# Recurrent features: the bonus issued last, the key products on VectorE, the inverse's turning held behind the turned keys' product

## The chip, the cores and the metric

The kernel runs on one core of a Trainium2 chip. The metric is the time of the whole program on the device in microseconds, the median of several runs. One core has a matrix engine (TensorE, in the traces PE, with its weight loads as PEld), VectorE (DVE), ScalarE (ACT), GpSimd (POOL) and SyncE (SP), which here only issues transfers. Each engine works through a queue of its own in order.

## The reference

The program is two residual blocks over a sequence of 512 positions and 1024 channels. The change lies in the second block's recurrent mixer (RWKV7), 1024 channels wide in 16 heads of 64:

```python
k_mod = k * (1.0 + (a - 1.0) * k_a)          # a = sigmoid(a0 + a_low @ a2)
kk = heads(k * k_k)
kk = kk / maximum(sqrt(sum(kk * kk)), 1e-12)

def step(state, inp):
    r_t, w_t, k_t, v_t, aa_t, bb_t = inp      # aa = -kk, bb = kk * a
    sa = einsum('bhvk,bhk->bhv', state, aa_t)
    state = state * w_t + sa * bb_t + v_t * k_t
    return state, einsum('bhvk,bhk->bhv', state, r_t)
_, y = lax.scan(step, state0, ...)
y = normalize(y) * lnx_w + lnx_b
bonus = sum(r_h * k_h * r_k, axis=-1, keepdims=True) * v_h
return (y + bonus) * g
```

Everything is float32.

## The kernel before

**GEMMs.** Both blocks are mostly GEMMs over 512 positions, kept at float32 accuracy by splitting operands into a high and a low part. One step is three matmuls of 128x512 (`mm3`, L193 to L195): high weights by high and by low activations, low weights by high activations. A weight chunk is transferred to `wraw` (L161, SP's queue), ScalarE makes its high part `whi` (L173) and VectorE the low part `wlo` (L174). `K.split` (L187, L188) makes such a pair of an activation, here `rkh` and `rkl` of `rk`.

**The recurrent mixer** (function `rwkv`) has eight tiles of 128 channels, two heads each. They are worked in four blocks of two: `features` for each of the two, then `inverse` and `chain` for the pair, then the outputs. The scan over 512 positions is done in chunks of 64: within a chunk the products of keys, reading vectors and decays form small matrices ("grams"), one triangular matrix is inverted, and `chain` carries the state from chunk to chunk.

`features(i)` loads k, r and v from scratch memory, makes the decays `pd` and their inverses `ip`, `tha` (a tanh from which a follows), `kk` and the norms `dd` (eight small matmuls L975, then L977). Then come, in this order of the code: `kw` (ScalarE, L980) and the modified key `km` = kw * k (GpSimd, L982); the bonus: `rk` (VectorE, L985), its split, two matmuls with a matrix of ones per head (L988), `bv` (L990, L991) and its transfer to scratch (L992), which the outputs read much later; `kka` = (0.5 tha + 0.5) * kk (ScalarE L994, GpSimd L995); the operands `ar` (L1005 to L1011) and `bk` (L1019, L1020) in two halves; the grams (PE L1030, masked into `g` by VectorE L1033); the turned keys: `bp` = bk times the chunk's decay (VectorE L1042), four transposes on PE (L1046), `bkt` (ScalarE L1048); the transposes of v (L1052) and `sv`.

`inverse` collects the diagonal 32x32 pieces of the grams of both features in `nst` by 32 copies on GpSimd (L1074), turns them on VectorE into `nn` (L1076), scales them by the norms (L1080), and does 31 pairs of small steps (L1088, L1090), all on VectorE; then `xsc` (L1092), `xn` (L1094) and `x0` (L1096). PE's L1117 needs `xn`.

**What sets the order.** A scheduler puts the instructions of the code in order for each engine, so that GEMMs of the mixer's inputs and of attention fill PE between the small recurrent matmuls. `K.behind(a, b)` makes a follow b in that order without a semaphore between them. The tiles of `features` are `bpage` tiles, 28 slots shared in turn. PSUM banks named `sc` (two) take the recurrent products.

Of the kernel before, what the change touches and what calls it, by code (L numbers as in the profile page):

```python
# [5 lines left out]
F32 = mybir.dt.float32  # L6
# [3 lines left out]
AF = mybir.ActivationFunctionType  # L10
ALU = mybir.AluOpType
AX = mybir.AxisListType
PSUM = bass.MemoryType.PSUM
P = 128
# [839 lines left out]
def rwkv(K, hs, filler=lambda: None):  # L854
    nc = K.nc
    c = K.const
# [7 lines left out]
    nc.vector.tensor_scalar(hw0, K.v("w0", 0, 8), 0.5, None, ALU.mult)  # L864
    omh = c.tile([P, 8], F32, name="omh")
    nc.vector.tensor_scalar(omh, hka, -1.0, 1.0, ALU.mult, ALU.add)
    half = c.tile([P, 1], F32, name="half")
    nc.vector.memset(half, 0.5)
    gneps = c.tile([P, 1], F32, name="gneps")
    nc.vector.memset(gneps, 64e-5)  # L870

# [46 lines left out]
    scr = K.dram.tile([DT, 2, P, S], F32, name="rw_scr")  # L918
    for i in range(2):
# [5 lines left out]
        for u in range(4):  # L925
            ps = K.mm()
# [3 lines left out]
            t = K.page(name="gt")  # L930
# [3 lines left out]
    def v3(ap, a, b):  # L934
        return ap.rearrange("p (a b) -> p a b", a=a)

    def features(i, dd, svs):
        o = Ctx()
        k = K.bpage(name="k")
        nc.sync.dma_start(k, zscr[i])  # L940
        r = K.bpage(name="r")
        nc.sync.dma_start(r, zscr[8 + i])
        v = K.bpage(name="v")
        nc.sync.dma_start(v, zscr[16 + i])

        ww = K.wload("w_w2", i, 2 * P, "l3", K.invp, los=((slice(0, 64), slice(P, 2 * P)),))
        ps = K.bank("sc")
        nc.tensor.matmul(ps, ww[:, :P], lwp, start=True, stop=False)
        nc.tensor.matmul(ps, ww[:, P:], lwp, start=False, stop=True)
        sg = K.bpage(name="sg")  # L950
        nc.scalar.activation(sg, ps, AF.Tanh, scale=0.5, bias=hw0[:, i:i + 1])
        nc.vector.tensor_scalar(sg, sg, 1.0, None, ALU.add)
        cs = K.bpage(name="cs")
        nc.vector.tensor_tensor_scan(cs, K.keep, sg, 0.0, ALU.mult, ALU.add)
        pd = K.bpage(name="pd")
        nc.scalar.activation(pd, cs, AF.Exp, scale=-0.5 * C05)
        ip = K.bpage(name="ip")
        nc.scalar.activation(ip, cs, AF.Exp, scale=0.5 * C05)
        wh, wl = K.wload("w_a2", i, P, "l2", K.invp)
        ps = K.bank("sc")  # L960
        nc.tensor.matmul(ps, wh, al, start=True, stop=False)
        nc.tensor.matmul(ps, wl, al, start=False, stop=True)
        tha = K.bpage(name="tha")
        nc.scalar.activation(tha, ps, AF.Tanh, scale=0.5, bias=ha0[:, i:i + 1])
        o.pl = K.sm.tile([P, 8], F32, name="pl", tag="pl")
        nc.vector.tensor_copy(o.pl, v3(pd, 8, 64)[:, :, 63])

        kk = K.bpage(name="kk")
        nc.scalar.activation(kk, k, AF.Copy, scale=K.v("k_k", i))
        sq = K.bpage(name="sq")  # L970
        nc.scalar.activation(sq, k, AF.Square, scale=K.v("k_k", i))
        ps = K.bank("sc")
        for j in range(8):
            bs = slice(64, 128) if j % 2 == 0 else slice(0, 64)
            nc.tensor.matmul(ps[bs, j // 2:j // 2 + 5:4], sq[:, j * 64:j * 64 + 64], K.hcol, start=True, stop=True)  # L975
        p8 = (i % 2) * 8
        nc.vector.tensor_scalar(dd[:, p8:p8 + 8], ps[:, 0:8], 1e-24, None, ALU.max)  # L977

        w = K.bpage(name="kw")
        nc.scalar.activation(w, tha, AF.Identity, scale=hka[:, i:i + 1], bias=omh[:, i:i + 1])  # L980
        km = K.bpage(name="km")
        nc.gpsimd.tensor_tensor(km, w, k, ALU.mult)  # L982

        rk = K.bpage(name="rk")
        nc.vector.scalar_tensor_tensor(rk, r, K.v("r_k", i), km, ALU.mult, ALU.mult)  # L985
        ps = K.bank("sc")
        for j, z in enumerate(K.split(rk, "rk", K.bpage)):
            nc.tensor.matmul(ps, K.bonr, z, start=(j == 0), stop=(j == 1))  # L988
        bv = K.bpage(name="bv")
        nc.vector.tensor_tensor(bv, ps, v, ALU.mult)  # L990
        nc.scalar.activation(bv, bv, AF.Identity, bias=K.v("lnx_b", i))  # L991
        nc.sync.dma_start(scr[i, 1], bv)  # L992
        kka = K.bpage(name="kka")
        nc.scalar.activation(kka, tha, AF.Identity, scale=0.5, bias=half)  # L994
        nc.gpsimd.tensor_tensor(kka, kka, kk, ALU.mult)  # L995

        o.ar, bk = [], []
        for hf in range(2):
            ts = slice(hf * 256, hf * 256 + 256)
            ar = K.bpage(name="ar")  # L1000
            a5 = ar.rearrange("p (j c x t) -> p j c x t", j=2, c=2, x=2)
            kk4, pd4, r4 = [z[:, ts].rearrange("p (j c t) -> p j c t", j=2, c=2) for z in (kk, pd, r)]
            for e in range(2):

                nc.vector.scalar_tensor_tensor(a5[:, :, e, 1 - e, 1:], kk4[:, :, e, 1:], -1.0, pd4[:, :, e, :63],  # L1005
                                               ALU.mult, ALU.mult)
                nc.vector.tensor_tensor(a5[:, :, e, e, :], r4[:, :, e], pd4[:, :, e], ALU.mult)
            ks_ = kk[:, ts].rearrange("p (j t) -> p j t", j=4)[:, :, 0:1]
            a4 = ar.rearrange("p (j t) -> p j t", j=4)
            nc.vector.tensor_scalar(a4[:, 0:4:2, 64:65], ks_[:, 0:4:2], -1.0, None, ALU.mult)  # L1010
            nc.vector.tensor_scalar(a4[:, 1:4:2, 0:1], ks_[:, 1:4:2], -1.0, None, ALU.mult)  # L1011
            o.ar.append(ar)
            b = K.bpage(name="bk")
            b5 = b.rearrange("p (j c x t) -> p j c x t", j=2, c=2, x=2)
            kka4 = kka[:, ts].rearrange("p (j c t) -> p j c t", j=2, c=2)
            km4 = km[:, ts].rearrange("p (j c t) -> p j c t", j=2, c=2)
            ip4 = ip[:, ts].rearrange("p (j c t) -> p j c t", j=2, c=2)
            for e in range(2):
                nc.vector.tensor_tensor(b5[:, :, e, 1 - e, :], kka4[:, :, e], ip4[:, :, e], ALU.mult)  # L1019
                nc.vector.tensor_tensor(b5[:, :, e, e, :], km4[:, :, e], ip4[:, :, e], ALU.mult)  # L1020
            bk.append(b)

        o.g = [[], []]
        for hf in range(2):
            pss = [K.bank("sc") for e in range(2)]
            for j in range(4):
                cl = slice(j * P, j * P + P)
                for e in range(2):
                    rows = slice(e * 64, e * 64 + 64)
                    nc.tensor.matmul(pss[e][:, cl], bk[hf][rows, cl], o.ar[hf][rows, cl], start=True, stop=True)  # L1030
            for e in range(2):
                g = K.bpage(name="g")
                nc.vector.tensor_tensor(v3(g, 2, 256), v3(pss[e], 2, 256),  # L1033
                                        K.gmask.rearrange("p (o t) -> p o t", o=1).broadcast_to([P, 2, 256]), ALU.mult)
                o.g[e].append(g)

        o.bkt = []
        for hf in range(2):
            tp = K.bank("sc")

            bp = K.bpage(name="bp")
            nc.vector.tensor_tensor(v3(bp, 4, P), v3(bk[hf], 4, P),  # L1042
                                    o.pl[:, hf * 4:hf * 4 + 4].rearrange("p (a o) -> p a o", o=1).broadcast_to([P, 4, P]),
                                    ALU.mult)
            for j in range(4):
                nc.tensor.transpose(tp[:, j * P:(j + 1) * P], bp[:, j * P:(j + 1) * P], K.idt)  # L1046
            t = K.bpage(name="bkt")
            nc.scalar.activation(t, tp, AF.Copy)  # L1048
            o.bkt.append(t)
        tp = K.bank("sc")  # L1050
        for m in range(4):
            nc.tensor.transpose(tp[:, m * P:(m + 1) * P], v[:, m * P:(m + 1) * P], K.idt)  # L1052
        for hf in range(2):

            t5 = svs[hf].rearrange("p (j c x n) -> p j c x n", j=2, c=2, x=2)[:, :, :, i % 2]
            src = v3(tp[:, hf * 256:hf * 256 + 256], 2, P)
            nc.scalar.activation(t5[0:64, :, 0, :], src[0:64], AF.Copy)
            nc.scalar.activation(t5[64:128, :, 1, :], src[64:128], AF.Copy)
        return o

    def inverse(os_, dd):

        ip_ = K.invp
        nst = ip_.tile([P, 32, 32], F32, name="nst", tag="nst")
# [8 lines left out]
                        cl = (q % 2) * 32  # L1073
                        nc.gpsimd.tensor_copy(nst[rows, u0:u0 + 2, :], g4[rows, :, 1 - q // 2, q // 2, cl:cl + 32])  # L1074
        nn = ip_.tile([P, 32, 32], F32, name="nn", tag="nn")
        nc.vector.transpose(nn, nst.rearrange("p u t -> p t u"))  # L1076
        rd = K.sm.tile([P, 32], F32, name="rd", tag="rd", bufs=2)
        nc.vector.transpose(rd, dd)
        nc.vector.reciprocal(rd, rd)
# [5 lines left out]
        for t in range(31):  # L1085
            n, w = 31 - t, t + 1
# [20 lines left out]
        for p_, o in enumerate(os_):  # L1107
            ps = K.bank("sc")
            t2 = K.bpage(name="t2")
            for ul in range(8):  # L1110
                e, jp = ul // 4, ul % 4
# [783 lines left out]
```

## Time and profile before

| what | value |
|---|---|
| median of 3 runs | 1985.5 us (1985.28 to 1989.89) |
| the profiled execution | 1986.21 us |
| its span, first to last instruction | 1984.4 us |
| TensorE busy | 1913.7 us (96%) |
| VectorE busy | 1270.7 us (64%) |
| ScalarE busy | 888.7 us (45%) |
| GpSimd busy | 92.5 us (5%) |
| mean granted TensorE clock | 0.993 of full |

The span leaves 1.8 us of the profiled execution outside. The recurrent stage lies between about 790 and 1420 us. In it PE is busy for 597.26 of 630.00 us; what ends its idle time there is named instruction by instruction in the list of waits.

### The profile page before, as it was taken

The page shows a single profiled execution, that of the slowest core. Times are in us where ns is not written, and L with a number is a line of the kernel's source. Part 1 is how long each engine was busy: PE and PEld are TensorE (multiplying, and loading weights), DVE is VectorE, ACT ScalarE, POOL GpSimd, SP SyncE. Part 2 cuts the span into 40 slices and gives each one's busy share as a digit, 9 for nine tenths or more (in the row PEclk, how much of TensorE's full clock was granted, in tenths as well). Part 3 has the DMA queues.
Part 4 walks back from the last instruction along what each step waited for, and adds up shares of the span by engine and source line. Part 5 has one row for each costly group of instructions (what it writes and reads, how often), then busy time and mean ns, then how long its engine had stood idle before and what let it go on. Part 6 is the DMA issues. An engine that isn't in the chain of part 4 may idle for free. (4 is left out here: it accounts for less than half of the span.)

```text
span 1984.4 us, 28608 instructions
## 1 busy us (share of the span) xinstructions
PE 1913.7 (96%) x10895; PEld 1558.5 (79%) x10907; DVE 1270.7 (64%) x2307; ACT 888.7 (45%) x1607; POOL 92.5 (5%) x207
## 2 busy tenths in 40 slices
PE   9999999999999999999999999989999899999998
PEld 7888887787888888777776777767767798888886
DVE  6746776868866668685575575575466566535654
ACT  5322233326655555534445555555642344423432
POOL 0000000000000000110020020020000000000002
PEclk9999999999999999999999999999999999999999
DMA  5332365675322223643542433433554603233222
GB/s 173 97 96 96 96 204 188 209 230 182 123 85 75 83 93 125 205 117 97 166 140 102 168 110 107 155 107 117 179 173 156 196 22 98 88 101 106 96 84 87
DMA packets 98377, 254.57 MB, mean 128 GB/s; under 512 B 11200, under 2 KB 15808, under 8 KB 98240
## 3 DMA queue, kind: packets, MB, share of 16 engines
q1 hardware_dynamic: 96640, 250.46, 39.3%
q8 instruction: 86, 1.41, 0.3%
q10 hardware_dynamic: 1376, 1.50, 0.2%
q0 software_dynamic: 224, 0.79, 0.1%
q14 instruction: 51, 0.42, 0.1%
HBM read 212.59 MB, written 37.75 MB: 126 GB/s over the span
## 5 line engine op out<-in xcount | busy, mean ns | idle before, releaser
L173 ACT ACTIVATE whi<-wraw 128x1024 fp32r<-128x1024 f32 (+4 forms) x293 | 289.7, 989 | 568.0 <-PE mm L194 351.9
L174 DVE TENSOR_TENSOR wlo<-wraw,whi 128x1024 fp32r<-128x1024 f32 (+4 forms) x293 | 332.0, 1134 | 198.3 <-ACT whi L173 194.2
L193 PE MATMUL mm<-hh,whi 128*128 128x512 f32 x936 | 373.1, 399 | 3.3 <-DVE cv L1554 2.4
L194 PE MATMUL mm<-hl,whi 128*128 128x512 f32 x936 | 375.6, 401 | 0.0
L195 PE MATMUL mm<-hh,wlo 128*128 128x512 f32 x936 | 372.2, 398 | 0.0
L193 PEld LDWEIGHTS mm<-hh,whi 128*128 128x128 f32 x936 | 176.8, 189 | 41.6 <-issue 4.4
L194 PEld LDWEIGHTS mm<-hl,whi 128*128 128x128 f32 x936 | 177.0, 189 | 37.8 <-issue 1.5
L195 PEld LDWEIGHTS mm<-hh,wlo 128*128 128x128 f32 x936 | 176.9, 189 | 36.0 <-issue 2.2
L194 PE MATMUL mm<-xgl,whi 128*128 128x512 f32 x416 | 163.5, 393 | 0.3 <-DVE xgl L386 0.3
L195 PE MATMUL mm<-xgh,wlo 128*128 128x512 f32 x416 | 162.1, 390 | 0.0
L193 PE MATMUL mm<-xgh,whi 128*128 128x512 f32 x416 | 161.8, 390 | 0.2 <-ACT xgh L385 0.2
L194 PE MATMUL mm<-yl,whi 128*128 128x512 f32 (+1 forms) x256 | 98.3, 384 | 0.0
L193 PE MATMUL mm<-yh,whi 128*128 128x512 f32 (+1 forms) x256 | 98.2, 383 | 0.0
L195 PE MATMUL mm<-yh,wlo 128*128 128x512 f32 (+1 forms) x256 | 98.1, 383 | 0.0
L194 PEld LDWEIGHTS mm<-xgl,whi 128*128 128x128 f32 x416 | 78.1, 188 | 17.3 <-issue 0.7
L195 PEld LDWEIGHTS mm<-xgh,wlo 128*128 128x128 f32 x416 | 78.1, 188 | 17.1 <-issue 0.7
L193 PEld LDWEIGHTS mm<-xgh,whi 128*128 128x128 f32 x416 | 78.1, 188 | 16.7 <-ACT xgh L385 0.6
L783 DVE SCALAR_TENSOR_TENSOR adaw<-adaw,cb 128x1024 f32<-128x1024 f32 x48 | 58.6, 1221 | 34.5 <-DMA adaw<-in_w_ada 33.0
L194 PE MATMUL mm<-fal,whi 128*128 128x512 f32 (+1 forms) x176 | 67.4, 383 | 0.0
L195 PE MATMUL mm<-fah,wlo 128*128 128x512 f32 (+1 forms) x176 | 67.3, 382 | 0.0
L193 PE MATMUL mm<-fah,whi 128*128 128x512 f32 (+1 forms) x176 | 67.3, 382 | 0.0
L720 ACT ACTIVATE p<-sc,nm 128x128 f32<-128x128 f32 (+1 forms) x64 | 33.7, 527 | 55.4 <-DVE nm L717 44.6
(450 smaller groups left out, 3690.5 us busy)
## 6 DMA issues: line engine op xcount, KB each, us to landing
adaw<-in_w_ada SPq DMA_DIRECT2D x48, 512.0 KB, 3.8
wraw<-in_w_up SPq DMA_DIRECT2D x41, 512.0 KB, 3.5
wraw<-in_w_at SPq DMA_DIRECT2D x36, 512.0 KB, 3.6
wraw<-in_w_pin SPq DMA_DIRECT2D x30, 512.0 KB, 3.6
wraw<-in_w_rw SPq DMA_DIRECT2D x27, 512.0 KB, 4.1
wraw<-in_w_min SPq DMA_DIRECT2D x22, 512.0 KB, 4.0
a_scr<-aqkv SPq DMA_DIRECT2D x36, 256.0 KB, 2.1
aq<-a_scr SPq DMA_DIRECT2D x36, 256.0 KB, 3.8
```

The lines of the kernel that those rows point to most:

```text
L173: a = nc.scalar.activation(hi, raw, AF.Copy)
L174: b = eng.tensor_tensor(lo, raw, f(hi), ALU.subtract)
L193: nc.tensor.matmul(out, wh, ah, start=first, stop=False)
L194: nc.tensor.matmul(out, wh, al, start=False, stop=False)
L195: nc.tensor.matmul(out, wl, ah, start=False, stop=last)
L720: nc.scalar.activation(p[:, :nk], sc[:, :nk], AF.Exp, bias=nm, scale=scale, accum_out=sm)
L783: nc.vector.scalar_tensor_tensor(w, w, 1.0, K.cb, ALU.mult, ALU.mult, accum_out=K.ada[:, i:i + 1])
```

## The change

Four edits, all in `rwkv`. The bonus (rk, its split, the two matmuls, bv and its transfer) is moved from the middle of `features` to its end. `km` is computed on VectorE and not on GpSimd. `kka` is one VectorE instruction, (tha + 1) * kk, in the place of one on ScalarE and one on GpSimd; its missing factor 0.5 moves into the product `bk`, which becomes a scalar_tensor_tensor, and the constant `half` goes. The turning `nn` in `inverse` is ordered behind the last `bp` of each of its two features (`o.turned`).

```diff
@@ features
         km = K.bpage(name="km")
-        nc.gpsimd.tensor_tensor(km, w, k, ALU.mult)
-
-        rk = K.bpage(name="rk")
-        nc.vector.scalar_tensor_tensor(rk, r, K.v("r_k", i), km, ALU.mult, ALU.mult)
-        ps = K.bank("sc")
-        for j, z in enumerate(K.split(rk, "rk", K.bpage)):
-            nc.tensor.matmul(ps, K.bonr, z, start=(j == 0), stop=(j == 1))
-        bv = K.bpage(name="bv")
-        nc.vector.tensor_tensor(bv, ps, v, ALU.mult)
-        nc.scalar.activation(bv, bv, AF.Identity, bias=K.v("lnx_b", i))
-        nc.sync.dma_start(scr[i, 1], bv)
+        nc.vector.tensor_tensor(km, w, k, ALU.mult)
+
         kka = K.bpage(name="kka")
-        nc.scalar.activation(kka, tha, AF.Identity, scale=0.5, bias=half)
-        nc.gpsimd.tensor_tensor(kka, kka, kk, ALU.mult)
+        nc.vector.scalar_tensor_tensor(kka, tha, 1.0, kk, ALU.add, ALU.mult)
...
-                nc.vector.tensor_tensor(b5[:, :, e, 1 - e, :], kka4[:, :, e], ip4[:, :, e], ALU.mult)
+                nc.vector.scalar_tensor_tensor(b5[:, :, e, 1 - e, :], kka4[:, :, e], 0.5, ip4[:, :, e], ALU.mult, ALU.mult)
...
-            nc.vector.tensor_tensor(v3(bp, 4, P), v3(bk[hf], 4, P),
+            o.turned = nc.vector.tensor_tensor(v3(bp, 4, P), v3(bk[hf], 4, P),
...
+        rk = K.bpage(name="rk")
+        nc.vector.scalar_tensor_tensor(rk, r, K.v("r_k", i), km, ALU.mult, ALU.mult)
+        ps = K.bank("sc")
+        for j, z in enumerate(K.split(rk, "rk", K.bpage)):
+            nc.tensor.matmul(ps, K.bonr, z, start=(j == 0), stop=(j == 1))
+        bv = K.bpage(name="bv")
+        nc.vector.tensor_tensor(bv, ps, v, ALU.mult)
+        nc.scalar.activation(bv, bv, AF.Identity, bias=K.v("lnx_b", i))
+        nc.sync.dma_start(scr[i, 1], bv)
         return o
@@ inverse
-        nc.vector.transpose(nn, nst.rearrange("p u t -> p t u"))
+        ins = nc.vector.transpose(nn, nst.rearrange("p u t -> p t u"))
+        for o in os_:
+            K.behind(ins, o.turned)
```

How the instructions stand on the engines follows from the scheduler. Three places, all in the second feature of block 2; rows show line, operation, output and inputs with buffer numbers.

VectorE around `nn`, before (the two `bp` are the two halves of the feature):

```order
L1033 TENSOR_TENSOR g_8929<-sc_8918,gmask_7324 128x512
L1042 TENSOR_TENSOR bp_8932<-bk_8886,pl_8843 128x512
L1076 STREAM_TRANSPOSE nn_8992<-nst_8958 128x1024
L1042 TENSOR_TENSOR bp_8941<-bk_8898,pl_8843 128x512
L1080 TENSOR_TENSOR nn_8992<-nn_8992,rd_8994 128x1024
L1088 TENSOR_TENSOR xtmp_9001<-nn_8992,xinv_8998 128x31
L1090 TENSOR_TENSOR xinv_8998<-xinv_8998,xtmp_9001 128x31
```

The same place now (lines are those of the changed kernel: L1030 is bp, L1074 nn, L1049 rk, L1054 bv):

```order
L1021 TENSOR_TENSOR g_8910<-sc_8899,gmask_7324 128x512
L1030 TENSOR_TENSOR bp_8913<-bk_8867,pl_8838 128x512
L174 TENSOR_TENSOR wlo_11603<-wraw_11600,whi_11602 128x1024
L1030 TENSOR_TENSOR bp_8922<-bk_8879,pl_8838 128x512
L1074 STREAM_TRANSPOSE nn_8986<-nst_8952 128x1024
L1049 SCALAR_TENSOR_TENSOR rk_8939<-r_8806,vec_72,km_8856 128x512
L1080 TENSOR_TENSOR nn_8986<-nn_8986,rd_8988 128x1024
L188 TENSOR_TENSOR rkl_8943<-rk_8939,rkh_8942 128x512
L1088 TENSOR_TENSOR xtmp_8995<-nn_8986,xinv_8992 128x31
L1171 COPY rh0_7607<-ch_9152 64x256
L1090 TENSOR_TENSOR xinv_8992<-xinv_8992,xtmp_8995 128x31
L1054 TENSOR_TENSOR bv_8948<-sc_8941,v_8808 128x512
```

The second bp stands ahead of nn with a weight split between the two, and rk, rkl and bv stand behind nn among the inverse's steps. In block 3 the two bp stood ahead of nn before too; there a wlo between them is gone. In block 1 a wlo and a `zm` (L882, a GEMM's output) now stand between the two bp, in block 4 a wlo.

PE from the second L1046 on, before (v's transposes are L1052, `ch` is the chain's first product):

```order
L1046 MATMUL sc_8940<-cst_84,bp_8941 128x128 x4
L1052 MATMUL sc_8949<-cst_84,v_8813 128x128 x4
L194 MATMUL mm_11575<-hl_7034,whi_11578 128x512
L195 MATMUL mm_11575<-hh_7033,wlo_11579 128x512
L193 MATMUL mm_11575<-hh_7035,whi_11578 128x512
L1157 MATMUL ch_9158<-sv_8654,g_8913 64x64
L1157 MATMUL ch_9158<-sv_8654,g_8915 64x64
L194 MATMUL mm_11575<-hl_7036,whi_11578 128x512
L195 MATMUL mm_11575<-hh_7035,wlo_11579 128x512
```

And now, from the transposes of v (here L1040) to the bonus's first matmul (here L1052):

```order
L1040 MATMUL sc_8930<-cst_84,v_8808 128x128 x4
L195 MATMUL mm_11565<-hh_7029,wlo_11569 128x512
L193 MATMUL mm_11565<-hh_7031,whi_11568 128x512
L194 MATMUL mm_11565<-hl_7032,whi_11568 128x512
L1157 MATMUL ch_9152<-sv_8650,g_8894 64x64
L1157 MATMUL ch_9152<-sv_8650,g_8896 64x64
L195 MATMUL mm_11565<-hh_7031,wlo_11569 128x512
L193 MATMUL mm_11565<-hh_7033,whi_11568 128x512
L194 MATMUL mm_11565<-hl_7034,whi_11568 128x512
L195 MATMUL mm_11565<-hh_7033,wlo_11569 128x512
L193 MATMUL mm_11565<-hh_7035,whi_11568 128x512
L1052 MATMUL sc_8941<-rkh_8942,bonr_7329 128x512
```

The bonus's matmuls come five GEMM matmuls behind L1157; before, they stood ahead of the grams. From the first L1046 to the first L1117 PE's order now holds 19, 11, 11 and 17 more GEMM matmuls in blocks 1 to 4.

VectorE from the norms to the operands of the grams, before:

```order
L977 TENSOR_SCALAR dd_8652<-sc_8849 128x8
L1078 STREAM_TRANSPOSE rd_8994<-dd_8652 128x32
L1079 RECIPROCAL rd_8994<-rd_8994 128x32
L985 SCALAR_TENSOR_TENSOR rk_8863<-r_8811,vec_72,km_8861 128x512
L174 TENSOR_TENSOR wlo_11579<-wraw_11576,whi_11578 128x1024
L188 TENSOR_TENSOR rkl_8867<-rk_8863,rkh_8866 128x512
L990 TENSOR_TENSOR bv_8872<-sc_8865,v_8813 128x512
L1005 SCALAR_TENSOR_TENSOR ar_8879<-kk_8845,pd_8828 128x2x63
```

And now (L980 is km, L983 kka, L993 the first ar):

```order
L975 TENSOR_SCALAR dd_8648<-sc_8844 128x8
L1078 STREAM_TRANSPOSE rd_8988<-dd_8648 128x32
L1079 RECIPROCAL rd_8988<-rd_8988 128x32
L980 TENSOR_TENSOR km_8856<-kw_8854,k_8804 128x512
L983 SCALAR_TENSOR_TENSOR kka_8858<-tha_8836,kk_8840 128x512
L174 TENSOR_TENSOR wlo_11569<-wraw_11566,whi_11568 128x1024
L993 SCALAR_TENSOR_TENSOR ar_8860<-kk_8840,pd_8823 128x2x63
```

km and kka stand where rk, rkl and bv stood.

## Rows read from the trace of the kernel before

**Rows 1.** Page, part 1: span, then busy time of each engine.

```profile
span 1984.4 us, 28608 instructions
...
PE 1913.7 (96%) x10895; PEld 1558.5 (79%) x10907; DVE 1270.7 (64%) x2307; ACT 888.7 (45%) x1607; POOL 92.5 (5%) x207
```

**Rows 2.** What PE waited for, 790 to 1420 us: total us, times, longest.

```profile
PE sc L1046 <- DVE bp L1042: 6.7, 3, 2.8
PE sc L1117 <- DVE xn L1094: 4.6, 4, 1.7
PE sc L1030 <- DVE bk L1020: 3.6, 5, 1.3
...
PE sc L988 <- ACT rkh L187: 2.4, 4, 0.9
...
PE sc L988 <- DVE rkl L188: 0.6, 1, 0.6
```

**Rows 3.** Timeline, block 2, second feature: start us, duration us, engine, line, [idle before].

```profile
1021.79 0.68 DVE L1042 TENSOR_TENSOR bp<-bk,pl 128x512 f32<-128x512 f32 x1
...
1023.98 0.39 PE L195 MATMUL mm<-hh,wlo 128*128 128x512 f32 x1
...
1024.20 0.40 PE L193 MATMUL mm<-hh,whi 128*128 128x512 f32 x1
1024.81 1.91 DVE L1076 STREAM_TRANSPOSE nn<-nst 128x1024 f32<-128x1024 f32 x1 [2.34 <-POOL nst L1074]
1026.63 0.66 DVE L1042 TENSOR_TENSOR bp<-bk,pl 128x512 f32<-128x512 f32 x1
...
1027.43 0.63 PE L1046 MATMUL sc<-cst,bp 128*128 128x128 f32 x4 [2.83 <-DVE bp L1042]
...
1029.51 0.50 PE L194 MATMUL mm<-hl,whi 128*128 128x512 f32 x1
```

**Rows 4.** Timelines of blocks 1 and 4, second features: PE, then VectorE.

```profile
867.00 0.63 PE L1046 MATMUL sc<-cst,bp 128*128 128x128 f32 x4 [2.06 <-DVE bp L1042]
...
1325.65 0.63 PE L1046 MATMUL sc<-cst,bp 128*128 128x128 f32 x4 [1.85 <-DVE bp L1042]
...
1320.79 0.67 DVE L1042 TENSOR_TENSOR bp<-bk,pl 128x512 f32<-128x512 f32 x1
1322.97 1.95 DVE L1076 STREAM_TRANSPOSE nn<-nst 128x1024 f32<-128x1024 f32 x1 [1.50 <-POOL nst L1074]
```

**Rows 5.** Copies into nst: beside bp, beside wlo; then all (lines view).

```profile
1021.91 0.66 POOL L1074 COPY nst<-g 32x64 f32<-32x64 f32 x1
...
1172.38 1.20 POOL L1074 COPY nst<-g 32x64 f32<-32x64 f32 x1
...
L1074 POOL COPY nst<-g 32x64 f32<-32x64 f32 x128 | 39.8, 311 | 45.3 <-DVE g L1033 40.4
```

**Rows 6.** Timelines of PE at the first L1117 of each block.

```profile
907.10 0.69 PE L1117 MATMUL sc<-xn,g 32*32 32x32 f32 x32 [1.69 <-DVE xn L1094]
...
1061.63 0.69 PE L1117 MATMUL sc<-xn,g 32*32 32x32 f32 x32 [0.92 <-DVE xn L1094]
...
1212.81 0.69 PE L1117 MATMUL sc<-xn,g 32*32 32x32 f32 x32 [0.98 <-DVE xn L1094]
...
1358.74 0.69 PE L1117 MATMUL sc<-xn,g 32*32 32x32 f32 x32 [1.03 <-DVE xn L1094]
```

**Rows 7.** Lines view, 790 to 1420 us: busy us, mean ns | idle before.

```profile
L982 POOL TENSOR_TENSOR km<-kw,k 128x512 f32<-128x512 f32 x8 | 11.0, 1374 | 137.4 <-ACT kw L980 93.6 <-DMA aq<-a_scr 24.5 <-DVE rd L1079 9.7
...
L1020 DVE TENSOR_TENSOR bk<-km,ip 128x128 f32<-128x128 f32 x32 | 8.9, 278 | 0.0
...
L985 DVE SCALAR_TENSOR_TENSOR rk<-r,vec,km 128x512 f32<-128x512 f32 x8 | 6.0, 751 | 8.1 <-POOL km L982 8.1
...
L990 DVE TENSOR_TENSOR bv<-sc,v 128x512 f32<-128x512 f32 x8 | 5.5, 690 | 5.2 <-PE sc L988 5.2
...
L187 ACT ACTIVATE rkh<-rk 128x512 fp32r<-128x512 f32 x8 | 5.0, 627 | 7.2 <-DVE rk L985 7.2
```

More of the change, by code (lines that the diff above doesn't have):

```diff
@@ L866, in rwkv @@
     nc.vector.tensor_scalar(omh, hka, -1.0, 1.0, ALU.mult, ALU.add)
-    half = c.tile([P, 1], F32, name="half")
-    nc.vector.memset(half, 0.5)
     gneps = c.tile([P, 1], F32, name="gneps")
```

## The prediction

> **What bounds the kernel now.** The page's first lines come first: TensorE is busy for 1913.7 of 1984.4 us, VectorE for 64% of the span [rows 1]. The change gives PE the same matmuls as before, so all that it can win or lose is PE's idle time, 70.7 us in the whole span, and of that only the idle time that ends at its own instructions. The second view is the list of what PE waited for between 790 and 1420 us, the recurrent stage [rows 2]. Five rows of it touch the change: L1046 waiting for bp 6.7 us (3 times), L1117 for xn 4.6 (4), L1030 for bk 3.6 (5), and L988 for rkh 2.4 and rkl 0.6 (5 in all). Together they are 17.9 us, 0.9% of the time: the ceiling of any gain here, and three times what a measurement of this kernel can tell from no change (0.3%, 6.0 us).
>
> The third view is the timeline of one such place [rows 3]. VectorE does bp for the first half at 1021.79, then its queue stands at nn, which waits for GpSimd's copies into nst and starts at 1024.81; the second bp, ready all along, is queued behind it and starts at 1026.63. PE had issued its last GEMM matmul at 1024.20 and sits at L1046 until 1027.43, 2.83 us. Block 1 (2.06) and block 4 (1.85) are the same picture [rows 4].
>
> **The change, part by part.** *The hold.* nn now stands behind both bp. In block 4 a weight split wlo and bp1 come directly after bp0, which starts at 1320.79 [rows 4], so bp1 ends 0.68 + 1.20 + 0.68 later even if wlo takes 1.20, at 1323.35, ahead of the time at which L1046 fell due (1325.65 - 1.85 = 1323.80). The same holds in block 2; in block 1 seven more GEMM matmuls come between the two L1046, 7 x 0.23 = 1.6 us (0.23 is the step from 1023.98 to 1024.20 in [rows 3]). The three stalls go: -6.7 us.
>
> *When nn can now start.* A copy of nst that meets bp on VectorE took 0.66 us, one that meets wlo 1.20, against a mean of 0.31 [rows 5]. So an instruction of VectorE put between bp0 and nn holds up GpSimd: bp1 by 0.66 - 0.31 = 0.35 us, a wlo by 0.89. By the order, blocks 1 and 4 get both (nn 1.24 later), block 2 gets bp1 alone (0.35; its wlo only moves), and block 3 loses the wlo it had (0.89 earlier). The Trainium skill, "SBUF — State Buffer", section "Who interferes with whom", says that a VectorE instruction with two SBUF inputs contends with a GpSimd instruction that reads SBUF, under an exclusive lock; the stretched copies of [rows 5] agree. By a lock that holds for the whole instruction the delays would be 0.7 and 1.2 us, and the sum below 1 to 2 us worse.
>
> *The bonus behind the inverse's start.* rk (0.75), rkl and bv (0.69 each) and their two L988 move to the end of the feature. In the first feature nothing else is queued there. In the second, rk stands behind nn. Block 2: nn from 1024.81 + 0.35 = 1025.16; the next instruction starts 1.82 later (as bp1 did, 1024.81 to 1026.63), then rk 0.75 and rkh on ScalarE 0.63 [rows 7]: 1028.36. PE without its stall starts the second L1046 one step after 1024.20, at 1024.43; L1046 to L1157 took 1029.51 - 1027.43 = 2.08, and five matmuls (1.13) stand before L988: due at 1027.64. New stall 0.7. Block 4 by the same working (L1046 could start at 1323.63, 0.17 ahead of the last matmul's end as in block 2, where the wait is counted from 1027.43 - 2.83 = 1024.60; L988 due 2.08 + 1.13 later, 1326.84; rkh ready 1322.97 + 1.24 + 1.82 + 0.75 + 0.63 = 1327.41): 0.6. Block 3, where attention's small transposes stand in the place of the five matmuls, I give the same 0.7 (an estimate); block 1 has 1.6 us more work in between: 0. New L988 stalls 2.0 in the place of the old 3.0, which all lay in the chain kw, km, rk, rkh that is now off that place: -1.0. Bounds: -3.0 (no new stall) and +1.5 (1.1 in each block).
>
> *km and kka on VectorE.* Eight products on GpSimd at 1.37 us and eight more like them end [rows 7]; 16 on VectorE begin, at 0.69 (bv) and 0.75 (rk): 11.5 us more for an engine at 64%. ScalarE loses eight kka activations. Neither engine is what PE waits for outside the rows above, so 0 by themselves; without that cover it would be at most the 11.5. What counts is the way from L975 to the first L1030. By the order it is now km, kka, four ar, and the first bk pair, 0.69 + 0.75 + 6 x 0.28 [rows 7] = 3.1 us. PE has 14 GEMM matmuls there in three features (3.2 us), 20 and 19 in two (4.4, with a wlo of 1.2 in the chain: 4.3 against 4.4), but in two others only 6 GEMM matmuls with 6 small ones of attention and 3 with 9, 2.1 and 1.7 us if a small one takes half a step. With 0.2 for the handover in the three and 0.1 in the two that gives 0.6 + 0.2 + 1.0 + 1.4 = 3.2 in the place of 3.6: -0.4. Bounds: -3.6 (all goes) and +1.5 (the features with 14 matmuls wait 0.8 each).
>
> *The inverse's path.* From nn to xn VectorE carries rk, rkl and bv in addition and, in blocks 1, 2 and 4, loses bp1: 2.13 - 0.68 = +1.45 us (block 3: +2.13). The order also puts a wlo (1.20) into block 2's stretch and two reductions of attention (some 0.69 each by bv's row) into block 4's. PE reaches L1117 earlier by the bp stall that went, later by the new L988 stall, and later by matmuls that the order now puts between the first L1046 and L1117: 19, 11, 11 and 17 of the GEMM and two L988 each, with attention's small ones added or gone: 4.8, 4.1, 1.7 and 4.0 us. So the xn stalls [rows 6] become, by block:
> 1: 1.69 + 2.06 - 0 - 4.8 + 1.24 + 1.45 = 1.6;
> 2: 0.92 + 2.83 - 0.7 - 4.1 + 0.35 + 2.65 = 1.95;
> 3: 0.98 - 0.7 - 1.7 - 0.89 + 2.13 = below 0, so 0;
> 4: 1.03 + 1.85 - 0.6 - 4.0 + 1.24 + 2.83 = 2.35.
> 5.9 in the place of 4.6: +1.3. Bounds -4.6 (none left) and +7.0 (1.75 more a block, all that nn could be held, 0.35 + 0.89, and half a us of contention with the 62 small steps).
>
> *Without a price.* rkh comes ahead of a whi on ScalarE in the second feature and can delay it by 0.63; that is covered by the GEMM's two weight buffers, and would be 2.5 us if it were not. The bonus's output on SP's queue now goes between the next feature's r and v; v is first read at that feature's L1052 and bv, so 0.
>
> Sum: -6.7 - 1.0 - 0.4 + 1.3 = -6.8 us. Against the profiled execution (1986.2, which is 1984.4 and 1.8 around it) that is 1979.4; the median is 0.7 below that execution. So 1985.5 - 6.8 = **1978.7**, its own range 1975 to 1982.
>
> **Rivals.** *Nothing takes the place of what goes.* If the freed GpSimd copies are no later and the new order gives PE cover at L988 and L1030, the bp, L988 and bk stalls all go and xn keeps its 4.6: -6.7 - 3.0 - 3.6 = -13.3, 1972. For it: the extra matmuls ahead of L1117, and km's latency of 1.37 halved. Against: rk queued behind a 1.9 us transposition that itself waits.
>
> *The stall moves on.* The inverse's path stays as late as it was, and PE, early at L1046, waits for the same nn at L988 and for xn. If new L988 stalls are 1.1 a block (4.4), xn 2.5 a block (10) and bk as before, the sum is -6.7 + 1.4 + 5.4 = 0.1: 1985.6, no change. For it: in all three blocks nn and not bp ends the chain, and it is not made faster. Against: 4.0 to 4.8 us of further PE work in those blocks. The Trainium skill, "Perfetto Trace Analysis", section "Optimizing Scalar/DVE Operations", warns that moving work between GpSimd and VectorE might not help since they share a read port. The stretched copies bear it out for bp and wlo; as this rival it gets its chance.
>
> *Slower.* One mechanism: VectorE's queue around nn is so full (bp, wlo, zm, bp, then rk, rkl, bv among the small steps) that xn comes later by more than PE's new cover. Each us beyond the working above costs PE a us in blocks 1, 2 and 4. From 4.3 us a block on (3 x 4.3 = 12.9, of which 6.8 eat the gain and 6 show) it is slower by 0.3%, 1991.5. For it: two further weight splits in the queue with no gap. Against: the working has 1.3 for the whole term.
>
> **How the numbers follow.** Forecast 0.42, nothing takes its place 0.18, moves on 0.30, slower 0.10. The time is that of the first, 1978.7. The range reaches to the second's 1972 with 1 us to spare, 1971, and to the third's 1985.6 with 2.4 for its uneven blocks, 1988; what is left out is the slower case and the tails. Faster by over 0.3% (below 1979.5) is the second and 0.30 of the first's 0.42: 0.48. Within 0.3%: the rest of the first and the third, 0.42. Slower 0.10.
>
> **What would show it.** After: L1046 without a wait for bp; L988 waiting for rkh in second features alone, about 2 us; L1030 for bk about 3.2; L1117 for xn near 6, none in block 3; GpSimd left with the copies and memsets; nn starting within 1.3 us of its old place behind the last g. Wrong would make it: xn waits above 10 us, L988 waits of over 1 us each, or bk waits that grow because PE reaches L1030 sooner than VectorE does two more products.

## The result

The changed kernel takes 1976.71 us (median of 6 runs, 1972.8 to 1980.52) against 1987.12 us before (6 runs, 1985.28 to 1995.21): a ratio of 0.9942, 95% interval 0.9925 to 0.9959, that is 11.5 us less (8 to 15); the two medians differ by 10.4. A second measurement, with runs of its own of both kernels, gave 0.9926 (0.9912 to 0.9939). A few executions that took over 5% longer than the others of their kernel are left out of all medians and ratios. The time forecast was 1978.7; the fall forecast was 6.8 us, less than the interval of the measured one holds.

The page of the profiled execution (1977.32 us), its first lines, which answer to [rows 1]:

```profile
span 1975.5 us, 28579 instructions
...
PE 1917.6 (97%) x10907; PEld 1560.2 (79%) x10907; DVE 1276.4 (65%) x2322; ACT 885.0 (45%) x1599; POOL 71.0 (4%) x191
```

The span is 8.9 us shorter than that of before. PE's idle time, span less busy, fell from 70.7 to 57.9 us, by 12.8; its busy time rose by 3.9 with the same matmuls. A part of both is a gap in the trace: that of before has 20 of the 32 matmuls L1326 (attention's mask), 10895 matmuls in all against 10907. Leaving the same twelve out of the changed kernel's trace lowers its busy time by 1.75 us, so the idle time of before is some 1.7 us too high (an estimate) and 69.0 is nearer. The rest of the difference is the clock, of which more below.

What PE waited for in the recurrent stage, 790 to 1420 us, in the changed kernel (total us, times, longest), beside [rows 2]:

```profile
PE sc L1117 <- DVE xn L1094: 4.4, 3, 2.0
PE sc L973 <- ACT sq L969: 4.1, 4, 2.7
PE tr L1392 <- DMA aq<-a_scr: 2.1, 2, 1.5
...
PE tr L1357 <- ACT ap L1350: 1.8, 4, 0.6
PE sc L1052 <- ACT rkh L187: 1.6, 3, 0.7
...
PE sc L1034 <- DVE bp L1030: 0.2, 1, 0.2
```

L1034 is the old L1046: its wait for bp is 0.2 us and was 6.7. The wait for bk, 3.6 before, has no row any more. The bonus's matmuls, now L1052, wait 1.6 and waited 3.0. The wait for xn is 4.4 and was 4.6. The wait for sq is 4.1, and a wait of attention for a transfer, 2.1 us, is new. The row for sq before (L975 is now L973):

```profile
PE sc L975 <- ACT sq L971: 1.7, 5, 0.6
```

Block 2's second feature, the place of [rows 3], in the timeline of the changed kernel:

```profile
1018.31 0.68 DVE L1030 TENSOR_TENSOR bp<-bk,pl 128x512 f32<-128x512 f32 x1
...
1019.06 1.23 DVE L174 TENSOR_TENSOR wlo<-wraw,whi 128x1024 fp32r<-128x1024 f32 x1
...
1020.21 0.72 DVE L1030 TENSOR_TENSOR bp<-bk,pl 128x512 f32<-128x512 f32 x1
...
1021.08 0.63 PE L1034 MATMUL sc<-cst,bp 128*128 128x128 f32 x4
...
1021.87 2.03 DVE L1074 STREAM_TRANSPOSE nn<-nst 128x1024 f32<-128x1024 f32 x1 [0.94 <-POOL nst L1072]
...
1023.83 0.71 DVE L1049 SCALAR_TENSOR_TENSOR rk<-r,vec,km 128x512 f32<-128x512 f32 x1
...
1025.25 0.50 PE L1052 MATMUL sc<-rkh,bonr 128*128 128x512 f32 x1 [0.68 <-ACT rkh L187]
```

The second bp is done before PE gets to L1034 at 1021.08, which shows no wait. nn waits 0.94 us for GpSimd's copies, rk follows 1.96 behind nn, and PE waits 0.68 us at the bonus's first matmul: the working gave 0.7 for this place. Block 1 had none, block 4 0.69 and block 3 0.27, where 0, 0.6 and, as an estimate, 0.7 were given.

### The profile page after: what moved, and what is told of

Read it like the earlier page. It is cut to its first block, busy times and chain, and to the rows that moved or that the text cites. A ratio compares the mean times of both kernels' runs of the same rounds, so it can differ in the third digit from the quotient of the medians.

```text
span 1975.5 us, 28579 instructions
## 1 busy us (share of the span) xinstructions
PE 1917.6 (97%) x10907; PEld 1560.2 (79%) x10907; DVE 1276.4 (65%) x2322; ACT 885.0 (45%) x1599; POOL 71.0 (4%) x191
```

## The experiments

Three edits can be made or left: H, the hold; B, the bonus last; P, the products on VectorE. All eight combinations were run. The table has the ratio to before and the profiled execution's PE idle time (span less busy, from the page).

To read it one place far from the edits has to be known: the combining of attention's three groups (function `att_combine`) behind the recurrent stage, here called the merging. It has twelve matmuls of its own, L1460 in the changed kernel, and in the kernel before and in the changed one each has GEMM matmuls on both sides in PE's order. Where several stand side by side instead, PE waits there for VectorE and the granted clock falls. The 40 us from at most 1 us ahead of the first of the twelve, by windows, for all three edits, P, then B with P, then H with P (PE's busy time is the second number, the granted clock the third from the end):

```profile
1466.00:1506.00 40.00, 39.82 (x154) 27.91 (x154) 30.10 (x45) 10.83 (x16) 0.00 (x0) 1.00 0.61 188
...
1480.00:1520.00 40.00, 34.67 (x118) 23.63 (x118) 28.06 (x43) 8.03 (x12) 0.00 (x0) 0.83 0.57 174
...
1472.00:1512.00 40.00, 37.52 (x134) 25.98 (x133) 28.68 (x43) 9.14 (x14) 0.00 (x0) 0.91 0.58 178
...
1473.00:1513.00 40.00, 37.06 (x131) 25.50 (x131) 28.28 (x42) 8.75 (x13) 0.00 (x0) 0.91 0.60 178
```

PE is idle there for 0.2, 5.3, 2.5 and 2.9 us; in the other kernels of the table it is idle for 0.2 at most, at a clock of 1.00. The column "outside the merging" leaves these 40 us out, and takes off the 1.7 us of the twelve records that the traces of before, e5 and e6 lack.

| kernel | ratio, 95% interval | PE idle, us | outside the merging | clock in the merging | wait for bp | for bk | for xn |
|---|---|---|---|---|---|---|---|
| before | 1 | 70.7 | 69.0 | 1.00 | 6.7 | 3.6 | 4.6 |
| H (e1) | 1.0002 (0.9991 to 1.0012) | 65.7 | 65.5 | 1.00 | none | 2.4 | 5.8 |
| B (e2) | 1.0047 (1.0028 to 1.0066) | 72.6 | 72.6 | 1.00 | 7.6 | 12.8 | 4.8 |
| P (e3) | 1.0009 (0.9996 to 1.0021) | 66.1 | 60.8 | 0.83 | 7.6 | none | 4.1 |
| B, P (e4) | 0.9962 (0.9947 to 0.9977) | 60.4 | 57.9 | 0.91 | 7.1 | none | 3.8 |
| B, H (e5) | 1.0003 (0.9985 to 1.0021) | 68.3 | 66.6 | 1.00 | none | 13.2 | 5.2 |
| H, P (e6) | 0.9975 (0.9959 to 0.9991) | 62.5 | 57.9 | 0.91 | none | none | 5.2 |
| all three | 0.9942, again 0.9926 | 57.9, again 57.1 | 57.7, again 56.9 | 1.00 | 0.2 | none | 4.4 |

(In e3 a part of the wait at the transposes of bp, 2.1 us, is named after a small step queued ahead of it on VectorE; it is counted with bp.)

Outside the merging the edits do not simply add up. The products alone take 8.2 us off PE's idle time and the hold alone 3.5, while the bonus last alone adds 3.6. On top of the products, the bonus last or the hold takes 2.9 more, and both together only 3.1 to 3.9. In time the changed kernel is ahead of e4 and e6 mostly by what those two lose in the merging: 2.5 and 2.9 us of idle time and 40 x 0.09 = 3.6 us each of clock, a part of it at the same moments. These are single profiles; the two of the changed kernel differ by 0.8.

**e1, the hold alone.**

```diff
-            nc.vector.tensor_tensor(v3(bp, 4, P), v3(bk[hf], 4, P),
+            o.turned = nc.vector.tensor_tensor(v3(bp, 4, P), v3(bk[hf], 4, P),
...
+        ins = nc.vector.transpose(nn, nst.rearrange("p u t -> p t u"))
+        for o in os_:
+            K.behind(ins, o.turned)
```

> The kernel before with the hold alone (nn ordered behind both bp). Theory A (each edit takes away its own waits, and the cover is there): the wait at L1046 for bp falls from 6.7 us to under 0.5, xn rises by no more than 2 us, ratio 0.997 (about 6 us less). Theory B (the stall only moves on to the next instruction that needs nn): bp goes, but the wait for xn rises by 4 us or more, ratio 0.999 to 1.000.

The wait for bp went, xn rose by 1.2 us, within what theory A allowed, and PE's idle time fell by 5.0 us, 3.3 without the missing records. The time did not fall: 1.0002, which is theory B's time without its wait, so neither theory came out whole. Rows of its list of waits:

```profile
PE sc L1119 <- DVE xn L1096: 5.8, 3, 2.9
PE sc L975 <- ACT sq L971: 3.5, 4, 2.4
...
PE sc L1030 <- DVE bk L1020: 2.4, 4, 1.0
...
PE tr L1328 <- ACT ap L1352: 2.3, 1, 2.3
```

Part of the 6.7 us came back at sq (1.7 before) and at attention's L1328 (0.6 before, there L1326). Of the 3.3 us that are left, about 2 went as clock: its runs had a median of 0.990 against 0.991 before. The remaining 1 us is less than the interval of the ratio can tell from nothing.

**e2, the bonus last alone.** The block of the bonus is cut out and pasted in at the end of features, as in the diff above; the products stay on GpSimd and the hold is left out.

> The kernel before with the bonus moved to the end of features, products still on GpSimd, no hold. Theory A: the waits for bk (3.6 us) and at the old place of the bonus's matmuls (3.0) fall together by about 5 us, bp stays at 5 to 7 us, ratio 0.997 to 0.998. Theory B: the bonus's matmuls wait behind nn for 4 us or more and eat what bk gives, ratio 1.000.

Neither came true. It is 9 us slower, the bonus's matmuls wait 0.3 us, and the wait for bk grew from 3.6 to 12.8 us. The longest of these waits in the timeline (L982 and L986 are GpSimd's km and kka, L996 and L998 the products ar, L1021 the first grams):

```profile
1290.83 1.28 POOL L982 TENSOR_TENSOR km<-kw,k 128x512 f32<-128x512 f32 x1 [21.43 <-ACT kw L980]
...
1291.34 0.92 DVE L996 SCALAR_TENSOR_TENSOR ar<-kk,pd 128x126 f32<-128x126 f32 x1
...
1293.66 1.69 POOL L986 TENSOR_TENSOR kka<-kka,kk 128x512 f32<-128x512 f32 x1 [1.55 <-ACT kka L985]
...
1294.14 1.35 DVE L998 TENSOR_TENSOR ar<-r,pd 128x128 f32<-128x128 f32 x1
...
1295.42 0.28 DVE L996 SCALAR_TENSOR_TENSOR ar<-kk,pd 128x126 f32<-128x126 f32 x1
...
1296.50 0.59 PE L1021 MATMUL sc<-ar,bk 64*128 64x128 f32 x2 [4.40 <-DVE bk L1011]
```

PE comes to the grams without the bonus's matmuls and their GEMM filling ahead of it (3 GEMM matmuls stand between the norms and the grams of this feature, before 13 and the bonus's two), and waits 4.40 us. Ahead of bk stand two products on GpSimd one after the other, and each holds up VectorE as well: an ar that meets km takes 0.92 us, one that meets kka 1.35, the next one, alone, 0.28. Over the stage the two forms of ar have a mean of 554 and 480 ns in e2, 282 and 281 in the changed kernel. The Trainium skill, "SBUF — State Buffer", section "Who interferes with whom", has it that a VectorE instruction with two SBUF inputs and a GpSimd instruction that reads SBUF exclude each other; the two stretched rows agree, here with VectorE as the one that is held up.

The wait for bk explains only a part of the 9 us. It grew by 9.2, but PE's idle time in all by 3.6, since other waits shrank. The rest is clock: the runs of e2 have a median of 0.987 against 0.991 for the kernel before beside them, some 8 us of 2000.

**e3, the products alone.**

```diff
-        nc.gpsimd.tensor_tensor(km, w, k, ALU.mult)
+        nc.vector.tensor_tensor(km, w, k, ALU.mult)
...
-        nc.scalar.activation(kka, tha, AF.Identity, scale=0.5, bias=half)
-        nc.gpsimd.tensor_tensor(kka, kka, kk, ALU.mult)
+        nc.vector.scalar_tensor_tensor(kka, tha, 1.0, kk, ALU.add, ALU.mult)
```

> The kernel before with km and kka on VectorE alone. Theory A: the way to bk is shorter by 1 to 2 us a feature, the wait for bk falls from 3.6 to about 1.5 us, bp and xn stay, ratio 0.998 to 0.999. Theory B (the bonus in VectorE's queue, not GpSimd's products, makes bk late): bk stays above 3 us, ratio 1.000.

The wait for bk went altogether, idle time fell by 4.6 us (2.9 without the missing records), and the time is the same. The merging shows the loss, by windows (busy us of the engines, then the granted clock), with its row of the list of waits; L1457 is this kernel's L1460:

```profile
1485.00:1505.00 20.00, 14.67 (x36) 8.62 (x37) 14.56 (x23) 3.04 (x6) 0.00 (x0) 0.66 0.63 191
...
PE sc L1457 <- DVE am L1461: 4.9, 4, 2.5
```

and the same piece of work in the kernel before:

```profile
1476.00:1496.00 20.00, 20.00 (x71) 12.44 (x71) 14.48 (x22) 4.00 (x6) 0.00 (x0) 1.00 0.63 208
```

A granted clock of 0.66 over 20 us, part at 2.4 and part at 1.2 GHz, against 1.00 is 20 x 0.34 = 6.8 us lost, beside the 5.3 us in which PE is idle. In e3's order half of the twelve matmuls stand side by side, and 23 GEMM matmuls stand among the twelve where before there are 72. The others come earlier: 4645 GEMM matmuls precede the first of the twelve, 4597 before and in the changed kernel.

**e4, all but the hold.**

```diff
-        for o in os_:
-            K.behind(ins, o.turned)
```

> The changed kernel without the hold. Theory A: the wait for bp comes back with 5 to 7 us, the ones for bk stay gone, ratio to before 0.997 (6 us more than the changed kernel). Theory B: PE loses at bp what it loses at L988 and xn in the changed kernel, ratio to before 0.994 as with the hold.

The wait for bp is back with 7.1 us, and the ratio is 0.9962, 4 us (0.2%) more than with the hold in the first measurement, where the two intervals overlap, and 7 us by the second. That is theory A by the waits for bp and bk and by the time. But the time is not that of the wait: outside the merging PE's idle time is 57.9 us, against 57.7 and 56.9 with the hold, because with it sq, the bonus's matmuls and xn take 2.4, 1.4 and 0.6 us more. There theory B is nearer. Three of e4's twelve matmuls of the merging stand side by side, and that place makes most of the difference in time.

**e5, the products back on GpSimd** in the changed kernel (the edit of e3 undone).

> The changed kernel with km and kka back on GpSimd and ScalarE: bonus last and hold, old products. Theory C (the bonus's matmuls and VectorE steps ahead of the grams were the cover of GpSimd's two products; moving them bares the products, so the move pays only with the products on VectorE): the wait for bk is 8 us or more, bp stays under 1 us, ratio to before 1.000 to 1.004. Theory D (the order that the scheduler makes differs by chance, and the move of the bonus alone had bad luck): bk under 5 us and ratio 0.997 or less, as the hold's 6 us would give.

Theory C: the wait for bk is 13.2 us, bp has no row, the ratio is 1.0003. The merging is whole here, as in e2, so the bared products are no matter of that place.

**e6, the bonus back in its old place** in the changed kernel.

> The changed kernel with the bonus back in its old place: hold and products on VectorE. Theory C: bk, being covered and short, waits under 1 us, the old waits of the bonus's matmuls for rkh of 2 to 3 us stay, bp under 0.5, ratio to before 0.996 to 0.998, between the changed kernel and the one before. Theory D: anything from 0.994 to 1.002, with the waits of other lines making the difference.

Theory C again by its numbers: 0.9975, no wait for bk, the bonus's matmuls wait 2.2 us. But theory D is not out: its merging ran at a granted clock of 0.66 from 1490 to 1500, 3.4 us, PE was idle there for 2.9, and outside it PE's idle time is 57.9, as in the changed kernel.

**e7, rk ahead of nn.** In the changed kernel nn is ordered behind rk (and so behind both bp):

```diff
-        nc.vector.scalar_tensor_tensor(rk, r, K.v("r_k", i), km, ALU.mult, ALU.mult)
+        o.turned = nc.vector.scalar_tensor_tensor(rk, r, K.v("r_k", i), km, ALU.mult, ALU.mult)
```

> The changed kernel with nn ordered behind rk of both features (and so behind both bp), in the place of behind bp. Theory A: rk no longer waits behind nn, the 1.6 us at the bonus's matmuls go, and xn comes at most 0.5 us later in each block because nn waits for GpSimd's copies anyway: ratio to before 0.993 to 0.995. Theory B: each 0.7 us of rk ahead of nn shows at xn, xn rises by 2 to 3 us, ratio 0.995 to 0.996.

The 1.6 us at the bonus's matmuls went and xn rose by 0.5 only, as theory A said, but the ratio is 0.9969, worse than either theory gave. The list of waits and the window of the merging bear on why:

```profile
PE tr L1357 <- ACT ap L1350: 5.1, 5, 2.0
PE sc L1117 <- DVE xn L1094: 4.9, 4, 2.0
```

```profile
1480.00:1495.00 15.00, 11.57 (x28) 6.59 (x26) 9.44 (x15) 1.89 (x3) 0.00 (x0) 0.66 0.68 209
```

Attention's L1357 waits 5.1 us where it waited 1.8, but sq takes 1.8 less, and outside the merging PE's idle time is 57.7 us (63.0 on the page, less 3.6 in the merging and 1.7 for the missing records), as in the changed kernel. In the merging three of the twelve stand side by side: 3.6 us of idle time, and 15 x 0.34 = 5.1 us to the clock. Over the whole of this profile the clock is no lower than in the changed kernel's (0.992 and 0.991); over its ten runs the median is, 0.9885.

**e8, the norms first.** kk, sq, the matmuls of the norms and dd are written ahead of the decays in features, in the changed kernel.

> The changed kernel with kk, sq and the norms' matmuls, which need k alone, written ahead of the decays in features. Theory A: the 4.1 us that PE waits for sq go, nothing takes their place: ratio to before 0.992 to 0.993. Theory B: the sum of waits stays, since ScalarE's queue ahead of tha and kw is as long as before and the wait comes back at bk: ratio 0.994 to 0.995.

Neither: 15 us slower than before. The wait for sq fell from 4.1 to 3.1 us only, and the merging fell apart (waits of PE from 1420 to 1530 us, then a window of it):

```profile
PE sc L1460 <- DVE w L1453: 16.0, 2, 14.5
PE sc L1460 <- DVE am L1464: 5.6, 5, 2.5
```

```profile
1480.00:1510.00 30.00, 10.42 (x17) 5.12 (x18) 25.94 (x38) 5.93 (x10) 0.00 (x0) 0.50 0.37 110
```

Eleven of the twelve L1460 stand side by side in its order, with 12 GEMM matmuls among the twelve. PE waits 21.6 us for VectorE there and runs what it has at 1.2 GHz (0.50).

**e9, every second copy on ScalarE**, in the changed kernel.

```diff
-                        nc.gpsimd.tensor_copy(nst[rows, u0:u0 + 2, :], g4[rows, :, 1 - q // 2, q // 2, cl:cl + 32])
+                        src = g4[rows, :, 1 - q // 2, q // 2, cl:cl + 32]
+                        if q % 2:
+                            nc.scalar.activation(nst[rows, u0:u0 + 2, :], src, AF.Copy)
+                        else:
+                            nc.gpsimd.tensor_copy(nst[rows, u0:u0 + 2, :], src)
```

> The changed kernel with every second copy into nst on ScalarE in the place of GpSimd. Theory E (the last copies on GpSimd, stretched by VectorE's bp and wlo, set when nn can start, and nn sets the waits at the bonus's matmuls and at xn): nn starts 0.5 to 1.5 us earlier behind the last g, the wait for rkh falls from 1.6 to under 0.8 and the one for xn from 4.4 to about 3, ratio to before 0.9925 to 0.9935. Theory F (the inverse's small steps among VectorE's other work set xn, and ScalarE's copies only delay rkh and the transposes' copies): xn stays above 4, ratio 0.994 to 0.996.

Half of each. In block 2 nn starts 0.65 us behind the second bp's start with no wait (1023.09 against 1022.44; in the changed kernel 1021.87 against 1020.21), and the bonus's matmuls do not wait; in all they wait 0.3, in block 3. So the copies did set nn there. But the waits for xn are 4.5 us as before. In block 3 nn starts 1.1 us earlier behind the last g and loses it again on the way to xn (37.7 us against 36.7); in block 4 xn comes 0.9 us earlier behind the last g, and so does PE, whose wait of 0.69 at the bonus is gone. The ratio is 0.9924 (0.9911 to 0.9936), median 1976.94, where the changed kernel measured beside it had 0.9926 and 1977.71: the same within the measurement.

**e10, sq ahead of kk** on ScalarE, in the changed kernel (the two activations trade places).

> The changed kernel with sq and kk in the other order on ScalarE, so that the square that the norms' matmuls wait for is one activation (0.6 us) earlier. Theory A: the four waits for sq (2.7, 0.6, 0.5, 0.4) lose 0.6 each, 4.1 falls to about 2.1, the rest of the stage stays: 2 us less than the changed kernel, ratio to before 0.993. Theory B: PE arrives at bk or at the next place so much earlier and waits there: ratio 0.994 as without.

The wait for sq fell by 0.9 us, not 2, and attention's transfers and L1368 took up as much; 0.9943 (0.9928 to 0.9957), not faster: theory B by the time.

**e11, the changed kernel again.**

> The changed kernel once more, as the measure for the two others on the same chip. Ratio to before 0.994 by the first measurement (0.9925 to 0.9959); the theory that its lead over the single edits was one good chip would have it at 0.997.

0.9926 (0.9912 to 0.9939): the lead is not that of one good chip.

**e12, the second feature's bonus behind the inverse**, on top of e9.

```diff
+        def bonus():
             rk = K.bpage(name="rk")
...
+        o.bonus = bonus
+        if i % 2 == 0:
+            bonus()
         return o
...
         xt = inverse(os_, dd)
+        os_[1].bonus()
```

> The kernel with every second copy on ScalarE, and in addition the second feature's bonus issued behind the inverse, so that rk, rkl and bv are out of VectorE's way between nn and xn. Theory G (those three, 2.1 us, are what xn is late by): from nn to xn each block is about 2 us shorter than in the changed kernel, the wait for xn falls from 4.5 to under 2 us, ratio to before 0.990 to 0.992. Theory H (PE's fewer matmuls ahead of L1117 bring it there earlier by as much, or the bonus's matmuls wait in the chain instead): the waits for xn stay above 3.5 us or the chain's grow by as much, ratio 0.992 to 0.994.

```profile
PE sc L973 <- ACT sq L969: 5.4, 6, 3.2
PE tr L1366 <- ACT ap L1359: 5.0, 5, 1.6
PE sc L1125 <- DVE xn L1102: 4.9, 3, 2.5
```

Theory H. xn (at L1125 here) comes earlier behind nn, in block 1 by 3.4 us (38.6 us from nn's start to xn's, 42.0 in e9), yet the waits for it are 4.9 us: the order has PE there earlier too, with less GEMM work ahead of it (177 GEMM matmuls between the last g and L1125 in block 1, 190 in e9). The waits for sq and attention (L1366) rose to 5.4 and 5.0. 0.9945 (0.9926 to 0.9964), not better.

## Why the prediction was right, point by point

The time was right, within 2.0 us, and the sum was made of the wrong terms. The forecast fall of 6.8 us is below the 8 to 15 that were measured. It came that near because the hold was priced too high and the products too low, and the time came nearer still because the forecast started from a median of before that is 1.6 us under the later one. That is luck.

- **The hold, -6.7.** Right as a wait: 6.7 became 0.2, and e4 brings 7.1 back. Wrong as a price: of PE's idle time outside the merging the hold takes 3.5 us in the kernel before (e1, no measurable time), 2.9 with the products, and 0.2 to 1.0 in the changed kernel. The rest of the wait comes back elsewhere. The 4 to 7 us of time between e4 and the changed kernel lie mostly in the merging.
- **When nn can start.** The stretched copies are real, and e9 shows that in block 2 they bind. In blocks 2, 3 and 4 nn starts 0.54 us later, 0.97 earlier and 1.26 later behind the last g than before, by the working 0.35 later, 0.89 earlier and 1.24 later. (The mean copy of 0.31 us that the working subtracts holds the stretched ones; by the median of 0.23 a bp costs 0.43 and a wlo 0.97.) In block 1 it is 2.12 where 1.24 was worked out, and for another reason, which VectorE's timeline there shows:

```profile
860.73 0.68 DVE L1030 TENSOR_TENSOR bp<-bk,pl 128x512 f32<-128x512 f32 x1
862.63 1.23 DVE L174 TENSOR_TENSOR wlo<-wraw,whi 128x1024 fp32r<-128x1024 f32 x1 [1.22 <-ACT whi L173]
...
864.43 0.68 DVE L1030 TENSOR_TENSOR bp<-bk,pl 128x512 f32<-128x512 f32 x1
865.03 2.04 DVE L1074 STREAM_TRANSPOSE nn<-nst 128x1024 f32<-128x1024 f32 x1
```

The wlo that the order puts between the two bp waits 1.22 us for ScalarE's whi, and bp and nn are queued behind it. nn waits for no copy there.
- **The bonus behind nn, 2.0 in the place of 3.0.** Measured 1.6, block by block as worked out but for block 3, which I had only estimated (0.27 where I gave 0.7).
- **The products, 3.2 in the place of 3.6.** This is the term that failed most. The wait for bk went entirely, in e3, e4 and e6 too, and the products alone take 8.2 us off PE's idle time outside the merging. The way from km to the first bk pair was worked out as 3.1 us from whole durations and took 2.6 (850.63 to 853.23 in block 1): queued instructions start 0.20 us apart where the row says 0.28 for one, and with GpSimd out of it no ar is stretched. Four of VectorE's rows there:

```profile
850.63 0.65 DVE L980 TENSOR_TENSOR km<-kw,k 128x512 f32<-128x512 f32 x1
...
852.00 0.28 DVE L995 TENSOR_TENSOR ar<-r,pd 128x128 f32<-128x128 f32 x1
852.20 0.28 DVE L993 SCALAR_TENSOR_TENSOR ar<-kk,pd 128x126 f32<-128x126 f32 x1
...
852.95 0.29 DVE L1008 TENSOR_TENSOR bk<-km,ip 128x128 f32<-128x128 f32 x1
```

(The three features with 14 matmuls come to 3.1 + 0.2 - 3.2 = 0.1 each by the working's own numbers, not 0.2.)
- **What the edits have to do with each other** is in no term. With the products on GpSimd the bonus was what covered them, and moving it bares them: bk waits 12.8 us in e2 and 13.2 in e5. That half is shown. The other half, that the move pays once the products are on VectorE, is shown only without the hold: 2.9 us of idle time outside the merging (e3 to e4). With the hold it is 0.2 to 1.0 (e6 to all three). In time the same steps are 9 us (0.47% by the ratios) and 7 to 10 us, but e3, e4 and e6 lose time in the merging and the changed kernel does not. Whether moving the bonus is what keeps the merging whole was not tried by itself; e4 has it moved and loses time there too.
- **The inverse's path, 5.9 in the place of 4.6.** Measured 4.4 in all, but 2.0, 0, 1.56 and 0.87 by block where 1.6, 1.95, 0 and 2.35 were worked out. nn to xn grew by 1.3, 2.0, 1.1 and 1.9 us (worked out 1.45, 2.65, 2.13, 2.83). What was off is PE's side. In block 2 attention's transposition waited 1.52 us for a transfer shortly ahead of L1117; in block 3 a wait of attention fell from 1.87 to 0.43, and PE came sooner. A balance of PE against VectorE over 40 us adds up every other wait in between; by block it held to about 2 us, no better.
- **Without a price.** The wait for sq, 1.7 to 4.1, was in no term. Its longest, 2.69 us at 1275.95, stands where the new order puts eight of attention's exponentials on ScalarE ahead of and among the decays of block 4.
- **The rivals.** The stall did not move on to L988 and xn; what came anew (sq 2.4, the transfer 2.1) came at places that the change does not touch. Still that rival has the hold nearly right: without it (e4) sq waits 1.7, the bonus 0.2 and xn 3.8, with it 4.1, 1.6 and 4.4. The mechanism of "nothing takes the place of what goes" is nearest for the wait for bk at L1030, and its 13.3 us lies inside the interval of what was measured.

## What to carry to other kernels

An instruction that only fills a gap is also cover: before moving it, ask what it covers, and shorten that first or in the same change. When a scheduler makes the order, one edit shifts GEMM filling and small transposes everywhere, so judge an edit by the waits it names, by PE's idle time over the whole page, and by the last place where the filling is used, not by one time; compare times only where that last place is the same in both. A wait taken away is worth its length only if the same work is not given a new wait, or a slower clock, somewhere else.

## What the runs showed of the hardware

**The clock is most of the spread.** The six runs of the changed kernel go from 1972.8 us at a mean granted clock of 0.992 to 1980.52 at 0.989, and 28 runs of the kernel before, measured together, from 1985.29 at 0.993 to 1999.37 at 0.986. Two stretches of the changed kernel's profile, each right behind a long wait of PE (2.01 us for xn at 909, 2.69 for sq at 1275):

```profile
910.00:917.00 7.00, 6.97 (x78) 5.51 (x78) 2.73 (x3) 6.20 (x12) 0.53 (x1) 0.55 0.27 66
...
1275.00:1282.00 7.00, 5.46 (x42) 4.31 (x44) 4.87 (x23) 3.86 (x7) 0.00 (x0) 0.57 0.57 199
```

Nearly all of these seven us ran at 1.2 GHz; they cost 7 x 0.45 + 7 x 0.43 = 6.2 us. The profile of before has three stretches of its own in the recurrent stage, 3 x 5 x 0.34 = 5.1 us:

```profile
1070.00:1075.00 5.00, 5.00 (x43) 3.35 (x36) 1.33 (x4) 2.98 (x13) 1.11 (x2) 0.66 0.20 52
...
1193.00:1198.00 5.00, 4.99 (x30) 3.88 (x31) 4.62 (x12) 1.58 (x3) 0.00 (x0) 0.66 0.57 157
...
1360.00:1365.00 5.00, 4.68 (x74) 3.80 (x73) 3.00 (x5) 4.62 (x9) 0.00 (x0) 0.66 0.02 5
```

Over the whole span the mean granted clock is 0.993 before and 0.991 after, 13.9 and 17.8 us short of full speed. Those 3.9 us, of which some fall into waits of PE and cost nothing, and the 1.7 us of missing records go together to make 12.8 us less idle into 8.9 us less span. After the first of the changed kernel's two long waits the clock fell in the second profile of the same program too (0.50 from 915 to 920); the wait of 1.69 us at the same place before was not followed by it. What decides it was not tried.

**A fallen clock far from the edit.** How many of the merging's twelve matmuls stand side by side goes with what is lost there. In the nine profiles in which none do (before, the changed kernel twice, e1, e2, e5, e9, e10, e12), 72 or 73 GEMM matmuls stand among the twelve, the granted clock is 1.00 over the 40 us, and PE waits there for 0.2 us at most. In e4, e6 and e7 three do, with 48 to 51 GEMM matmuls; the clock is 0.91, 0.91 and 0.87, and PE waits 1.9, 2.0 and 3.6 us for VectorE. In e3 six do, with 23: 0.83 and 4.9 us. In e8 eleven do, with 12: 0.57 and 21.6 us. That the missing filling is the cause is argued from this; no run changed it alone.
